# Last down projection of a decoder layer as seven block products, with the block sums of its weights added up in DRAM

## The chip, the core and the metric

The kernel runs on one core of a Trainium2 chip, as one program in float32 with split operands (below). The metric is the time of one execution on the device in microseconds.

## The reference, cut to what matters

The layer is SwiGLU feed-forward, mixers, SwiGLU feed-forward, each with RMS norms before and after and a residual. With 512 tokens, a width of 1024 and 2816 features, the last part is

```python
def swiglu(x, w_gate, w_up, w_down):
    return (jax.nn.silu(x @ w_gate) * (x @ w_up)) @ w_down

h = swiglu(rms_norm(x, ffn2_pre_norm[l]), ffn2_w_gate[l], ffn2_w_up[l], ffn2_w_down[l])
x = x + 0.5 * rms_norm(h, ffn2_post_norm[l])
```

The change concerns the product with `w_down` of this second feed-forward. Its left operand H is 512 x 2816, its right one 2816 x 1024.

## The kernel before, in words

Every float32 product is made of three TensorE matmuls: an operand x is split into `hi`, a copy cast to the format that TensorE reads, and `lo`, the rest x - hi; the product is hi.hi + lo.hi + hi.lo (`mm3`). ScalarE makes `hi` and VectorE makes `lo`, for weights in `wload` (L105 load by SP's queue, L106 cast, L109 rest) and for H in `split` (L122, L123).

The stages in order of time: the first feed-forward's gate and up products, its down projection, the mixers, the second feed-forward's gate and up products, its down projection, and the ending. In each gate-and-up stage most of the feature tiles run in `fast_phase` (16 of 22 tiles): for each tile gate and up are computed together as seven block products of 128x256 (`fast_prods`, matmuls on L437), on sums of weight blocks that VectorE makes in SBUF (`fast_load`, L403 to L417). The raw weights of a tile are four loads of 256 KB into one of two buffers `fq`; the split sums go into one of two sets (`fset`, and `fxth` with `fxtl`). The loads of tile f + 2 are issued as the buffer of tile f comes free.

The last down projection is plain: two parts of two token blocks (128 tokens each), each part with two column halves of 512, and each of these with 22 feature tiles (`down_half`). In the first column half of a part, H is split tile by tile as it is used. The weights are loaded again for each part, 4 x 22 loads of 256 KB. Six of them go through a small pool, the others through a ring of eight in the memory of two old tiles (`ringr`, `ringh`). The four sums of a part are in four PSUM banks. x, the residual, is loaded at the start of the stage by four DMAs of 512 KB, and the gain of the norm (`gb`) during the first part. `ending` takes the sums of one token block: two squares with row sums on ScalarE, two products with the gain and a chain of 128x1 instructions on VectorE, two updates of x (L171) and two stores (L172). In the second part, the second token block's last eight tiles come after the first block's last, so that the first block's ending runs beside them.

The order on each engine is that of the program, except that a scheduler moves instructions whose inputs are there earlier ahead of others by its own estimate. On the chip each engine then executes in that order, and an instruction that waits holds what is queued behind it. `order` adds to the scheduler's constraints that one instruction stands after another. A tile of a pool that reuses the memory of an older tile waits until every reader of the older one is done.

Of the kernel before, what the change touches and what calls it, by code (L numbers as in the profile page):

```python
# [10 lines left out]
F32 = mybir.dt.float32  # L11
# [6 lines left out]
P = 128  # L18
D = 1024
KT = 8  # L20
# [19 lines left out]
class Body:  # L40
# [74 lines left out]
    def mm3(self, out, lh, ll, rh, rl, first, last):  # L115
        t = self.nc.tensor
        t.matmul(out, lh, rh, start=first, stop=False)  # L117
        t.matmul(out, ll, rh, start=False, stop=False)  # L118
        t.matmul(out, lh, rl, start=False, stop=last)  # L119
# [299 lines left out]
    def fast_tile(self, f, S, T, banks, s7, H):  # L419
        g, up = self.fast_prods(S, T, banks, s7)  # L420
# [4 lines left out]
    def fast_prods(self, S, T, banks, s7, mid=()):  # L425
# [6 lines left out]
        def prod(out, w, t, start=False):  # L432
            th, tl = T[t]
            for k in range(4):
# [5 lines left out]
                m(wh, tl[:, k], start=False, stop=k == 3)  # L440
# [21 lines left out]
    def fast_phase(self, n, f0, xh, xl, RB, H, step):  # L462
# [12 lines left out]
        for f in range(f0 + 2, FT):  # L475
            i = f % 2
            self.fast_tile(f, self.sets[i], T, banks[i], s7[i], H)
# [37 lines left out]

    def load_x(self, src, x=None, after=None, tbs=range(TB), c=slice(0, D)):
# [9 lines left out]
    def order(self, later, earlier):  # L526
        d = mybir.DependencyInfo(mybir.DependencyClass.NoSync, mybir.DependencyReason.DATA)
# [645 lines left out]
    def run(self):  # L1173
# [3 lines left out]
        with tc.tile_pool(name="f1", bufs=1) as fp, contextlib.ExitStack() as x1:  # L1177
# [57 lines left out]
            with tc.tile_pool(name="st1", bufs=1) as st:  # L1235
# [4 lines left out]
                self.fast_phase(1, 4, xh, xl, RB, H, step)  # L1240
# [237 lines left out]
        with tc.tile_pool(name="f2", bufs=1) as fp, contextlib.ExitStack() as x1:  # L1478
# [26 lines left out]
            Hh, Hl, lor, gb = self.hidden_parts(x1, 2)  # L1505
            x = self.load_x(dx2)
            b4, c4 = self.bank8()
            self.ring = (self.cp.tile([P, KT, SEQ], F32, tag="xth", name="ringr"), self.cp.tile([P, KT, SEQ], F32R, tag="xtl", name="ringh"))
            self.ringi = -6
            parts = (((0, 1), [b4[:2], b4[2:]]), ((2, 3), [c4[:2], c4[2:]]))  # L1510
            lo4 = self.cp.tile([P, 4, 512], F32R, tag="mtl", name="lo4")
            lor += [lo4[:, i] for i in range(4)]
            for tbs, acc in parts:
                for h in range(2):
                    t0 = tbs[0] * P
                    step = (lambda k: self.hsplit(H, Hh, Hl, k, slice(t0, t0 + 256))) if h == 0 else None
                    self.down_half(Hh, Hl, "ffn2_d", FT, tbs, acc[h], h, lor if h and t0 else (), step, t0)
            self.post_gain("ffn2_post", 0.5 * self.RK, gb)
# [3 lines left out]
            for tbs, acc in parts:  # L1522
                for i, b in enumerate(tbs):
                    self.ending([acc[0][i], acc[1][i]], x, gb, b, self.out, tmp)
# [101 lines left out]
```

## Time and profile before

| | |
|---|---|
| median of 3 runs | 1325.09 us (1324.64 to 1326.45) |
| profiled execution, span from first to last instruction | 1326.1 us |
| TensorE busy | 1299.2 us, 98% |
| VectorE busy | 959.7 us, 72% |
| ScalarE busy | 738.6 us, 56% |
| GpSimd busy | 126.6 us, 10% |
| DMA | 178.35 MB, all but instruction loads from the queues of SP and ScalarE |

The profile gives no time of the profiled execution besides its span, which lies inside the range of the runs and 1.0 us above their median. Engine names in rows: PE is TensorE's matmuls, PEld its weight loads, DVE VectorE, ACT ScalarE, POOL GpSimd, SP SyncE, and a q behind a name is that engine's instruction queue or DMA issue. Lnnn is a line of the kernel.

### The profile page before, as it was taken

The page shows a single profiled execution, that of the slowest core. Times are in us where ns is not written, and L with a number is a line of the kernel's source. Part 1 is how long each engine was busy: PE and PEld are TensorE (multiplying, and loading weights), DVE is VectorE, ACT ScalarE, POOL GpSimd, SP SyncE. Part 2 cuts the span into 40 slices and gives each one's busy share as a digit, 9 for nine tenths or more (in the row PEclk, how much of TensorE's full clock was granted, in tenths as well). Part 3 has the DMA queues.
Part 4 walks back from the last instruction along what each step waited for, and adds up shares of the span by engine and source line. Part 5 has one row for each costly group of instructions (what it writes and reads, how often), then busy time and mean ns, then how long its engine had stood idle before and what let it go on. Part 6 is the DMA issues. An engine that isn't in the chain of part 4 may idle for free. (4 is left out here: it accounts for less than half of the span.)

```text
span 1326.1 us, 22368 instructions
## 1 busy us (share of the span) xinstructions
PE 1299.2 (98%) x8091; PEld 1129.2 (85%) x8091; DVE 959.7 (72%) x1860; ACT 738.6 (56%) x1591; POOL 126.6 (10%) x113
## 2 busy tenths in 40 slices
PE   8999999999999999999999999999999999999997
PEld 7889999888887778888777788888788999998886
DVE  6898786778567866755788766666687888756765
ACT  6566665767455644416565456444685566646642
POOL 0020000000001221102111121223100000000000
PEclk8999999999999999999999999999999999999999
DMA  7653331577664342234221242333744433318673
GB/s 241 194 162 113 111 112 49 167 258 246 200 181 125 97 114 72 80 107 120 64 56 57 64 135 65 96 96 112 277 148 155 141 107 114 111 33 277 195 226 104
DMA packets 106302, 178.35 MB, mean 134 GB/s; under 512 B 18780, under 2 KB 28368, under 8 KB 106192
## 3 DMA queue, kind: packets, MB, share of 16 engines
q1 hardware_dynamic: 105904, 176.67, 42.8%
q8 instruction: 63, 1.03, 0.3%
q10 hardware_dynamic: 288, 0.26, 0.1%
q14 instruction: 47, 0.39, 0.1%
HBM read 166.84 MB, written 10.01 MB: 133 GB/s over the span
## 5 line engine op out<-in xcount | busy, mean ns | idle before, releaser
L106 ACT CAST whi<-wraw 128x512 fp32r<-128x512 f32 (+1 forms) x286 | 173.6, 617 | 157.0 <-PE pfm L119 58.5
L109 DVE TENSOR_TENSOR wlo<-wraw,whi 128x512 fp32r<-128x512 f32 (+1 forms) x255 | 174.8, 694 | 70.3 <-ACT whi L106 65.7
L117 PE MATMUL pfm<-xth,whi 128*128 128x512 f32 x272 | 108.7, 405 | 0.9 <-DVE X L940 0.4
L118 PE MATMUL pfm<-xth,wlo 128*128 128x512 f32 x272 | 109.1, 406 | 0.0
L119 PE MATMUL pfm<-xtl,whi 128*128 128x512 f32 x272 | 108.3, 404 | 0.0
L106 ACT CAST ringh<-ringr 128x512 fp32r<-128x512 f32 x82 | 49.7, 621 | 42.9 <-DMA ringr<-in_ffn_d_dram 14.0
L437 PE MATMUL smm<-thi,fset 128*128 128x256 f32 x384 | 67.9, 276 | 0.0
L109 DVE TENSOR_TENSOR wlo<-ringr,ringh 128x512 fp32r<-128x512 f32 x75 | 51.3, 690 | 19.6 <-PE acc_e L119 8.0
L117 PEld LDWEIGHTS pfm<-xth,whi 128*128 128x128 f32 x272 | 51.3, 190 | 11.6 <-PE pfm L119 0.8
L109 POOL TENSOR_TENSOR wlo<-wraw,whi 128x512 fp32r<-128x512 f32 x28 | 38.1, 1360 | 229.2 <-ACT whi L106 165.1
L119 PEld LDWEIGHTS pfm<-xtl,whi 128*128 128x128 f32 x272 | 51.3, 190 | 9.8 <-issue 0.8
L118 PEld LDWEIGHTS pfm<-xth,wlo 128*128 128x128 f32 x272 | 51.3, 190 | 9.2 <-DVE wlo L109 0.4
L457 DVE TENSOR_TENSOR up<-s,smm 128x256 f32<-128x256 f32 x32 | 13.5, 422 | 61.8 <-ACT se L452 61.8
L437 PEld LDWEIGHTS smm<-thi,fset 128*128 128x128 f32 x384 | 57.9, 188 | 0.2
L437 PE MATMUL smm<-thi,fxtl 128*128 128x256 f32 x192 | 53.2, 277 | 0.6 <-DVE fxtl L412 0.6
L437 PE MATMUL smm<-thi,fxth 128*128 128x256 f32 x192 | 53.0, 276 | 0.0
L437 PE MATMUL se<-thi,fset 128*128 128x256 f32 x256 | 45.2, 276 | 0.0
L1058 ACT ACTIVATE Pm<-Pm,nm 128x384 f32<-128x384 f32 (+2 forms) x64 | 35.6, 558 | 14.5 <-DVE nm L1057 14.0
L123 DVE TENSOR_TENSOR Hl<-H,Hh 128x256 fp32r<-128x256 f32 x88 | 35.0, 421 | 8.6 <-ACT Hh L122 7.6
L403 DVE TENSOR_TENSOR fs<-fq 128x1024 f32<-128x1024 f32 x32 | 39.0, 1220 | 0.9 <-DMA fq<-in_ffn_u_dram 0.9
L437 PEld LDWEIGHTS se<-thi,fset 128*128 128x128 f32 x256 | 38.6, 188 | 0.0
L437 PEld LDWEIGHTS smm<-thi,fxtl 128*128 128x128 f32 x192 | 36.0, 188 | 1.0 <-DVE fxtl L412 1.0
(611 smaller groups left out, 4245.5 us busy)
## 6 DMA issues: line engine op xcount, KB each, us to landing
wraw<-in_ffn_d_dram SPq DMA_DIRECT2D x94, 256.0 KB, 2.8
ringr<-in_ffn_d_dram SPq DMA_DIRECT2D x82, 256.0 KB, 3.0
fq<-in_ffn_g_dram SPq DMA_DIRECT2D x64, 256.0 KB, 2.8
fq<-in_ffn_u_dram SPq DMA_DIRECT2D x64, 256.0 KB, 3.1
wraw<-in_ffn_g_dram SPq DMA_DIRECT2D x34, 256.0 KB, 3.2
wraw<-in_ffn_u_dram SPq DMA_DIRECT2D x34, 256.0 KB, 3.4
woraw<-in_w_out_dram SPq DMA_DIRECT2D x32, 256.0 KB, 4.4
mfq<-in_w_gate_dram SPq DMA_DIRECT2D x28, 256.0 KB, 3.0
```

What stands on the lines that cost most here:

```text
L106: nc.scalar.copy(hi, raw)
L109: eng.tensor_tensor(lo, raw, hi.bitcast(F32), op=OP.subtract)
L117: t.matmul(out, lh, rh, start=first, stop=False)
L118: t.matmul(out, ll, rh, start=False, stop=False)
L119: t.matmul(out, lh, rl, start=False, stop=last)
L123: return self.nc.vector.tensor_tensor(lo, src, hi.bitcast(F32), op=OP.subtract)
L403: add = lambda *x: v.tensor_tensor(*x, op=OP.add)
L437: m = lambda x, y, **kw: te.matmul(out, x, y, skip_group_check=True, **kw)
L457: v.tensor_tensor(up[:, 256:], s7, a, op=OP.subtract)
L1058: nc.scalar.activation(pm, pm, AF.Exp, bias=nm[:, qb : qb + 1], scale=-1.0, accum_out=sm[:, qb : qb + 1])
```

## The change

H and the weight W are cut into 2 x 2 blocks: token halves of 256, feature halves of 11 tiles, column halves of 512. Four sums T1 to T4 of weight blocks are made once, in DRAM, by DMAs issued from GpSimd: `weight_sums` lists eight steps, four plain copies and four that add into their destination, each cut into four pieces of 176 rows of 4 KB (704 KB). In the fast phase of the first feed-forward, a piece is handed out after the second and after the fifth product of each tile, with a wait for the last matmul of that product.

`down7` replaces the four `down_half` calls. It runs seven products of 256 tokens x 11 feature tiles x 512 columns. Three take a sum or difference of blocks of H as left operand: s3 into a buffer, s2 and s4 in place in H. Partial results move between PSUM banks by ScalarE copies, so that later products accumulate on them; two results are finished by VectorE additions into `c2` in SBUF. H is split in chunks of up to four tiles, the weights in pairs of tiles where they do not go through the small pool. The weights are now 7 x 11 tile loads, taken from W or from T1 to T4. x is loaded after the second product and the gain after the third, its second half with the sign turned. The endings of tokens 256 to 511 come after the sixth product, those of tokens 0 to 255 after the seventh.

```diff
@@ fast_prods
-                m(wh, tl[:, k], start=False, stop=k == 3)
+                self.mmark = m(wh, tl[:, k], start=False, stop=k == 3)
+            if side and w in (self.S_S3, self.S_S1):
+                side.pop(0)()
@@ fast_phase
-            self.fast_tile(f, self.sets[i], T, banks[i], s7[i], H)
+            self.fast_tile(f, self.sets[i], T, banks[i], s7[i], H, [side.pop(0) for _ in range(2) if side])
@@ new functions
+    def weight_sums(self, w, n):
+
+        g = self.nc.gpsimd
+        nh = self.a[w].shape[1] // 2
+        T = [self.dr.tile([nh, P, 512], F32, name=f"T{n}{i}") for i in range(4)]
+        v = lambda x: x.rearrange("k p n -> (k p n)").rearrange("(r c) -> r c", c=1024)
+        B = lambda i, j: v(self.a[w][j, nh * i : nh * i + nh])
+        t1, t2, t3, t4 = map(v, T)
+        todo = ((t1, B(0, 1), 0), (t3, B(1, 1), 0), (t1, B(0, 0), 1), (t3, B(0, 1), 1), (t2, t3, 0), (t2, B(0, 0), 1), (t4, t2, 0), (t4, B(1, 0), 1))
+
+        def piece(o, x, add, c):
+            i = g.dma_start(o[c], x[c], max_dma_last_dim=2048, **({"accum_op": OP.add} if add else {}))
+            self.order(i, self.mmark, mybir.DependencyClass.Sync)
+
+        r = nh * P // 8
+        return T, [lambda s=s, c=slice(r * j, r * j + r): piece(*s, c) for s in todo for j in range(4)]
+
+    def down7(self, H, w, T, x1, banks, done):
+
+        nc, v = self.nc, self.nc.vector
+        X, Y, Z, Q = banks
+        sh, sl = self.sring
+        sraw, q7, c2 = self.sraw, self.q7, self.c2
+        d = self.a[w]
+        nh = d.shape[1] // 2
+        h = lambda i, j, k, n: H[:, nh * j + k : nh * j + k + n, 256 * i : 256 * i + 256]
+        tt, st = v.tensor_tensor, v.scalar_tensor_tensor
+
+        def s3(k, n):
+            t = sraw[slot % 2][:, :n]
+            self.order(tt(t, h(0, 0, k, n), h(1, 0, k, n), op=OP.subtract), last)
+            return t
+
+        def s2(k, n):
+            a, q = h(0, 0, k, n), h(1, 0, k, n)
+            tt(q, h(1, 1, k, n), q, op=OP.subtract)
+            st(a, a, -1.0, q, op0=OP.mult, op1=OP.subtract)
+            return a
+
+        def s4(k, n):
+            a = h(0, 0, k, n)
+            st(a, a, -1.0, h(0, 1, k, n), op0=OP.mult, op1=OP.subtract)
+            return a
+
+        part = lambda i, j: lambda k, n: h(i, j, k, n)
+        seq = (
+            (X, d[0, :nh], part(0, 0), True),
+            (Q, T[2], s3, True),
+            (X, T[1], s2, False),
+            (Y, d[0, nh:], part(0, 1), False),
+            (Z, T[0], part(1, 0), False),
+            (X, T[3], part(1, 1), False),
+            (Z, d[1, nh:], s4, False),
+        )
+        slot = wslot = 0
+        last = None
+        wr, wh_, wl_ = self.wring
+
+        def weights(m, src, k):
+            nonlocal wslot
+            if m == 0 and k < 6:
+                return {k: self.wload(src[k])}
+            n = 2 if (nh - k) % 2 == 0 else 1
+            raw, hi, lo = wr[wslot % len(wr)][:, :n], wh_[wslot % len(wh_)][:, :n], wl_[wslot % len(wl_)][:, :n]
+            wslot += 1
+            nc.sync.dma_start(raw, src[k : k + n].rearrange("k p n -> p k n"))
+            nc.scalar.copy(hi, raw)
+            tt(lo, raw, hi.bitcast(F32), op=OP.subtract)
+            return {k + i: (hi[:, i], lo[:, i]) for i in range(n)}
+
+        for m, (acc, src, make, start) in enumerate(seq):
+            ops, ws = {}, {}
+            cuts = (0, 1, 4, 8, nh) if m == 0 else (0, 4, 8, nh)
+            lag = 8 if m == 6 else 0
+
+            def mm(i, k):
+                t = slice(i * P, i * P + P)
+                hi, lo = (o[:, t] for o in ops[k])
+                wh, wl = ws[k]
+                e = lambda a, b, s, f: nc.tensor.matmul(acc[i], a, b, start=s, stop=f, skip_group_check=True)
+                e(hi, wh, start and k == 0, False)
+                e(lo, wh, False, False)
+                self.mmark = e(hi, wl, False, k == nh - 1)
+
+            for k in range(nh):
+                if k in cuts:
+                    n = cuts[cuts.index(k) + 1] - k
+                    hi, lo = sh[slot % 4][:, :n], sl[slot % 4][:, :n]
+                    slot += 1
+                    f = make(k, n)
+                    nc.scalar.copy(hi, f)
+                    last = tt(lo, f, hi.bitcast(F32), op=OP.subtract)
+                    ops.update({k + i: (hi[:, i], lo[:, i]) for i in range(n)})
+                if k not in ws:
+                    ws.update(weights(m, src, k))
+                for i in range(1 if k >= nh - lag else 2):
+                    mm(i, k)
+            if lag:
+                for k in range(nh - lag, nh):
+                    mm(1, k)
+            for i in range(2):
+                if m == 0:
+                    nc.scalar.copy(Y[i], X[i])
+                elif m == 1:
+                    nc.scalar.copy(q7[:, i], Q[i])
+                elif m == 2:
+                    nc.scalar.copy(Z[i], X[i])
+                elif m == 4:
+                    tt(c2[:, 1, i], Z[i], q7[:, i], op=OP.add)
+                elif m == 5:
+                    tt(c2[:, 0, i], X[i], q7[:, i], op=OP.add)
+            done(m)
+
@@ first feed-forward
-                self.fast_phase(1, 4, xh, xl, RB, H, step)
+                self.T2, side = self.weight_sums("ffn2_d", 2)
+                self.fast_phase(1, 4, xh, xl, RB, H, step, side)
@@ last down projection
-            Hh, Hl, lor, gb = self.hidden_parts(x1, 2)
-            x = self.load_x(dx2)
+            dw = x1.enter_context(self.tc.tile_pool(name="dw2", bufs=1))
+            gb = dw.tile([P, 2, 512], F32, name="gb")
+            self.sraw = [dw.tile([P, 4, 256], F32, name=f"sraw{i}") for i in range(2)]
+            self.q7 = dw.tile([P, 2, 512], F32, name="q7")
+            self.c2 = dw.tile([P, 2, 2, 512], F32, name="c2")
+            lor = [dw.tile([P, 2, 512], F32R, name=f"lor{i}") for i in range(4)]
+            self.wx = None
+            dv = x1.enter_context(self.tc.tile_pool(name="dv2", bufs=1))
+            ch = lambda nm: dv.tile([P, 4, 256], F32R, name=nm)
+            sh2 = ch("sh2")
+            dv.tile([P, 64], F32, name="gap")
+            sh3, sl2, sl3 = ch("sh3"), ch("sl2"), ch("sl3")
+            dv.tile([P, 64], F32, name="gap2")
+            dv = x1.enter_context(self.tc.tile_pool(name="dz2", bufs=1))
+            sl0, sl1, sh0, sh1 = ch("sl0"), ch("sl1"), ch("sh0"), ch("sh1")
+            self.sring = [sh0, sh1, sh2, sh3], [sl0, sl1, sl2, sl3]
+            x = []
             b4, c4 = self.bank8()
-            self.ring = (self.cp.tile([P, KT, SEQ], F32, tag="xth", name="ringr"), self.cp.tile([P, KT, SEQ], F32R, tag="xtl", name="ringh"))
-            self.ringi = -6
-            parts = (((0, 1), [b4[:2], b4[2:]]), ((2, 3), [c4[:2], c4[2:]]))
+            banks = b4[:2], c4[:2], c4[2:], b4[2:]
+            rings = [self.cp.tile([P, KT, SEQ], t, tag=g, name=n) for t, g, n in ((F32, "xth", "ringr"), (F32R, "xtl", "ringh"))]
             lo4 = self.cp.tile([P, 4, 512], F32R, tag="mtl", name="lo4")
-            lor += [lo4[:, i] for i in range(4)]
-            for tbs, acc in parts:
-                for h in range(2):
-                    t0 = tbs[0] * P
-                    step = (lambda k: self.hsplit(H, Hh, Hl, k, slice(t0, t0 + 256))) if h == 0 else None
-                    self.down_half(Hh, Hl, "ffn2_d", FT, tbs, acc[h], h, lor if h and t0 else (), step, t0)
-            self.post_gain("ffn2_post", 0.5 * self.RK, gb)
+            two = lambda x: [x[:, i : i + 2] for i in range(0, x.shape[1], 2)]
+            self.wring = two(rings[0]), two(rings[1]), lor + two(lo4)
             pre = self.cp.tile([P, 4, 512], F32, tag="mth", name="pre")
             pre = iter([pre[:, i % 4] for i in range(8)])
             tmp = lambda: next(pre)
-            for tbs, acc in parts:
-                for i, b in enumerate(tbs):
-                    self.ending([acc[0][i], acc[1][i]], x, gb, b, self.out, tmp)
+
+            def done(m):
+                if m == 1:
+                    x.extend(self.load_x(dx2, after=self.mmark))
+                if m == 2:
+                    i = self.nc.sync.dma_start(gb.rearrange("p h d -> p (h d)"), self.a["ffn2_post"].partition_broadcast(P))
+                    self.order(i, self.mmark)
+                    for h in range(2):
+                        nc.vector.tensor_scalar(gb[:, h], gb[:, h], 0.5 * self.RK * (1, -1)[h], None, op0=OP.mult)
+                if m == 5:
+                    for i in range(2):
+                        self.ending([self.c2[:, 0, i], self.c2[:, 1, i]], x, gb, 2 + i, self.out, tmp)
+                if m == 6:
+                    for i in range(2):
+                        self.ending([banks[1][i], banks[2][i]], x, gb, i, self.out, tmp)
+
+            self.down7(H, "ffn2_d", self.T2, x1, banks, done)
 
 
 def host_layout(i):
```

In a piece, `self.order(i, self.mmark, Sync)` is a wait on the chip, where the other uses of `order` only fix the scheduler's order.

## Rows read from the trace of the kernel before

**Rows 1.** The page's first part: busy us, share of the span and instructions of an engine.

```profile
PE 1299.2 (98%) x8091; PEld 1129.2 (85%) x8091; DVE 959.7 (72%) x1860; ACT 738.6 (56%) x1591; POOL 126.6 (10%) x113
```

**Rows 2.** The stages one by one: length, busy us and instructions of each engine, granted clock, share of the DMA engines, GB/s. In order: gate and up of the first feed-forward, its down projection with what follows, gate and up of the second, its down projection, the tail.

```profile
85.50:242.00 156.50, 155.76 (x1353) 155.01 (x1351) 118.36 (x141) 91.29 (x188) 2.55 (x1) 1.00 0.31 97
242.00:371.00 129.00, 127.87 (x587) 105.08 (x588) 93.71 (x202) 85.60 (x181) 2.08 (x4) 1.00 0.74 230
1048.00:1198.00 150.00, 149.58 (x1312) 149.38 (x1310) 112.89 (x136) 86.62 (x178) 0.00 (x0) 1.00 0.31 99
1198.00:1318.40 120.40, 120.30 (x528) 98.88 (x528) 85.11 (x169) 67.89 (x143) 0.00 (x0) 1.00 0.68 205
1318.40:1326.10 7.70, 0.00 (x0) 0.00 (x0) 3.30 (x10) 0.69 (x2) 0.00 (x0) 0.74 0.29 110
```

**Rows 3.** The timeline of TensorE's matmuls at the start and the end of the last down projection: start, us, engine, line, operation, count, and in brackets the idle time before and what ended it.

```profile
1197.30 0.28 PE L437 MATMUL se<-txb,fxth 128*128 128x256 f32 x1
1198.00 0.73 PE L117 MATMUL acc_mm<-whi,Hh 128*128 128x512 f32 x2 [0.42 <-ACT Hh L122]
...
1317.75 0.39 PE L118 MATMUL acc_s<-ringh,Hl 128*128 128x512 f32 x1
1317.98 0.39 PE L119 MATMUL acc_s<-lo,Hh 128*128 128x512 f32 x1
```

**Rows 4.** DMA traffic from 100 to 209 us, inside the first fast gate-and-up stage: all packets, the queue of SP, and one of its two groups of loads with KB each and median us to landing.

```profile
DMA packets 6636, 12.23 MB, mean 112 GB/s; under 512 B 736, under 2 KB 736, under 8 KB 6624
q1 hardware_dynamic: 6624, 12.06, 34.8%
fq<-in_ffn_u_dram SPq DMA_DIRECT2D x24, 256.0 KB, 2.8
```

**Rows 5.** The timeline of VectorE and ScalarE around the start of the last down projection; a row with x2 or more is a run of instructions back to back.

```profile
1171.37 1.22 DVE L403 TENSOR_TENSOR fs<-fq 128x1024 f32<-128x1024 f32 x1
1172.50 1.22 DVE L417 TENSOR_TENSOR fset<-fq,fset 128x1024 fp32r<-128x1024 f32 x1
...
1181.72 1.23 DVE L417 TENSOR_TENSOR fxtl<-fq,fxth 128x1024 fp32r<-128x1024 f32 x1 [0.69 <-ACT fxth L416]
...
1202.26 3.11 DVE L123 TENSOR_TENSOR Hl<-H,Hh 128x256 fp32r<-128x256 f32 x9
...
1207.81 1.29 DVE L109 TENSOR_TENSOR wlo<-ringr,ringh 128x512 fp32r<-128x512 f32 x2
...
1201.37 3.17 ACT L122 CAST Hh<-H 128x256 fp32r<-128x256 f32 x10
...
1206.93 1.14 ACT L106 CAST ringh<-ringr 128x512 fp32r<-128x512 f32 x2
```

**Rows 6.** Waits between 1196 and 1326 us: engine and line that waited, for whom, us in total, times, the longest. The first row is all that TensorE waited.

```profile
PE acc_mm L117 <- ACT Hh L122: 0.4, 1, 0.4
...
DVE gb L254 <- DMA gb<-in_ffn_post_dram: 2.5, 1, 2.5
```

**Rows 7.** DMA traffic from 1190 to 1326.1 us: GB/s in 40 slices, and two groups of loads.

```profile
GB/s 0 199 247 379 402 319 233 229 306 159 274 191 222 179 117 243 196 214 211 183 163 236 230 302 339 187 202 194 217 172 195 194 210 164 0 0 2 154 0 154
...
ringr<-in_ffn_d_dram SPq DMA_DIRECT2D x82, 256.0 KB, 3.0
xa<-dx SPq DMA_DIRECT2D x2, 512.0 KB, 4.2
```

**Rows 8.** The timeline of GpSimd from 60 to 371 us: its last instruction in the first gate-and-up stage and the next one after it.

```profile
83.96 4.08 POOL L308 TENSOR_TENSOR sg<-sg,RB 128x256 f32<-128x256 f32 x1 [8.42 <-ACT sg L304]
307.70 1.84 POOL L933 MEMSET X<- 128x1024 f32 x2 [219.66 <-DVE Hl L123]
```

**Rows 9.** The timeline of SP, ScalarE and VectorE in the first fast stage: the ends of two tiles (L422), the last of the four loads of a tile (L406), the first use of that tile's weights (L409), the end of their conversion (L412), and the last load of the stage.

```profile
189.52 0.35 SPq L406 DMA_DIRECT2D fq<-in_ffn_u_dram  x1
...
208.65 0.39 SPq L406 DMA_DIRECT2D fq<-in_ffn_u_dram  x1
...
193.77 0.60 ACT L422 ACTIVATE sg<-se 128x512 f32<-128x512 f32 x1 [0.75 <-PE se L437]
...
195.45 0.63 ACT L409 CAST fxth<-fq 128x512 fp32r<-128x512 f32 x1
...
203.35 0.60 ACT L422 ACTIVATE sg<-se 128x512 f32<-128x512 f32 x1 [0.75 <-PE se L437]
...
202.97 1.75 DVE L412 TENSOR_TENSOR fxtl<-fq,fxth 128x1536 fp32r<-128x1536 f32 x1
```

**Rows 10.** The timeline of the ending of the last token block.

```profile
1318.46 0.60 ACT L164 ACTIVATE junk<-acc_s 128x512 bf16<-128x512 f32 x1 [4.23 <-PE acc_s L119]
...
1319.18 0.69 DVE L165 TENSOR_TENSOR pre<-acc_s,gb 128x512 f32<-128x512 f32 x1 [1.49 <-ACT junk L164]
...
1321.31 1.41 DVE L171 SCALAR_TENSOR_TENSOR xb<-pre,r1y,xb 128x512 f32<-128x512 f32 x2
```

More of the change, by code (lines that the diff above doesn't have):

```diff
@@ L118, in mm3 @@
         t.matmul(out, ll, rh, start=False, stop=False)
-        t.matmul(out, lh, rl, start=False, stop=last)
+        self.mmark = t.matmul(out, lh, rl, start=False, stop=last)
     def split(self, hi, lo, src):
@@ L417, in fast_load, with fast_tile @@
             v.tensor_tensor(lo[:, c], x, hi[:, c].bitcast(F32), op=OP.subtract)
-    def fast_tile(self, f, S, T, banks, s7, H):
-        g, up = self.fast_prods(S, T, banks, s7)
+    def fast_tile(self, f, S, T, banks, s7, H, side=()):
+        g, up = self.fast_prods(S, T, banks, s7, side=side)
         sg = self.tp.tile([P, SEQ], F32, tag="tmpa", bufs=2, name="sg")
@@ L423, in fast_tile, with fast_prods @@
         self.nc.vector.tensor_tensor(H[:, f], sg, up, op=OP.mult)
-    def fast_prods(self, S, T, banks, s7, mid=()):
+    def fast_prods(self, S, T, banks, s7, mid=(), side=()):
         nc, v, te = self.nc, self.nc.vector, self.nc.tensor
@@ L460, in fast_prods, with fast_phase @@
         return g, up
-    def fast_phase(self, n, f0, xh, xl, RB, H, step):
+    def fast_phase(self, n, f0, xh, xl, RB, H, step, side=()):
         quads, sums, s7 = self.fr
@@ L524, in load_x, with order @@
         return x
-    def order(self, later, earlier):
-        d = mybir.DependencyInfo(mybir.DependencyClass.NoSync, mybir.DependencyReason.DATA)
+    def order(self, later, earlier, how=mybir.DependencyClass.NoSync):
+        d = mybir.DependencyInfo(how, mybir.DependencyReason.DATA)
         self.tc.add_manual_dep(getattr(later, "ins", later), getattr(earlier, "ins", earlier).name, d, reason="order")
```

## The prediction

> **What bounds the kernel now.** I read the page's busy times first. TensorE is busy for nearly the whole span and GpSimd for a tenth of it [rows 1]. A busy TensorE proves little by itself, so the stages come next [rows 2]: in both fast gate-and-up stages and in the last down projection the TensorE column is within 1 us of the length of the stage, at the full granted clock (1.00, the 2.4 GHz level), while VectorE is busy 71 to 76% and ScalarE 56 to 58%. The timeline of TensorE at both ends of the down projection shows it without holes [rows 3]: a gap of 0.42 us before its first matmul, then one matmul on the next until 1318.37. So this stage is bound by the number of its matmuls: 120.30 us for 528, or 0.2278 us each, and what feeds them has room. Behind it lies a tail of 7.7 us with no matmul, the ending of the last token block [rows 10].
>
> **Fewer matmuls.** Before, there are 22 feature tiles x 4 token blocks x 2 column halves x 3 = 528 matmuls of 512 columns. After, 7 products x 11 tiles x 2 token blocks x 3 = 462 of the same shape. 66 x 0.2278 = 15.0 us less, all of it on the path that sets the end, as long as the operands come in time. The bounds of this term are narrow, since shape and clock do not change.
>
> **The start of the stage.** The 0.42 us before the first matmul is a wait for the cast of H [rows 3, 6], which stood behind other work. Now the first chunk of H has split buffers in the space of the raw weights, free once the weights of the last tile have been converted at 1182.95, some 14 us earlier [rows 5]. I take 0.4 us as gained; the bounds are 0 and 0.6.
>
> **VectorE in the down projection.** Back to back, instructions start closer than their duration: one of 256 elements each 0.34 us ((3.11 - 0.42)/8), of 512 each 0.60 (1.29 - 0.69), of 1024 each 1.13 (1172.50 - 1171.37) [rows 5]; scalar_tensor_tensor of 512 each 0.66 [rows 10], so 1.24 for 1024 by the same ratio. Products 2 to 7 each split weights in five pairs and a single, 5 x 1.13 + 0.60 = 6.25, and H in chunks of 4, 4 and 3 tiles, 1.13 + 1.13 + 0.87 = 3.13: 9.4 us. The first product takes 9.7 (7 x 0.60 + 2 x 1.13 for weights, 3.2 for four chunks). The formed operands add 3.1 us (product 2), 3.1 + 3.4 (product 3, two instructions per chunk) and 3.4 (product 7). Four sums into c2 cost 2.4, and two endings (tokens 256 to 511) now fall inside product 7: 0.6 + 3.5 us each by the last ending [rows 10], 8.2 in all. Together 9.7 + 56.4 + 13.0 + 2.4 + 8.2 = 89.7 us of 105.2, 85%, where before it was 71%. On totals VectorE does not become the bound.
>
> The tight place is product 3. By its last chunk VectorE must have done 9.7 + 12.5 + 15.9 = 38.1 us, and TensorE asks for that chunk at 2 x 15.0 + 8 x 6 x 0.2278 = 41.0 us after the start. That leaves 2.9 us, plus about 3.0 done ahead (chunks of one and three tiles, three weights). An operand goes VectorE, ScalarE, VectorE, so some of it goes in hand-overs. ScalarE needs 7.8 us per product (1024 elements at 0.94, from 0.31 for 256 and 0.52 for 512 [rows 5]) and two PSUM copies of 0.6 [rows 9]: no bound in 15.
>
> **Moved DMAs.** Weights stay at 77 x 256 KB = 20.2 MB in 105 us, 192 GB/s against the 205 of the stage now [rows 2]. Moved into it are the four loads of x (2.1 MB, issued before the weights until now), put on SP's queue after product 2, and the gain, after product 3. What stands behind them on SP are the weight loads. At the best rate in a slice, 402 GB/s, x takes 5.2 us [rows 7]; the weight rings hold four pairs, eight tiles, 8 x 1.37 = 10.9 us of matmuls. So it is hidden, and costs up to 5 us without that cover. The gain's scaling on VectorE waited 2.5 us for its DMA before [rows 6], with splits queued behind it; this can recur, after product 3, where VectorE has 5 us per product to spare. For all supply together the bounds are 0 and 9 us; I take 1.0, nearer to zero because the sums leave 5.9 us at the tightest place.
>
> **The weight sums in the first stage.** 32 pieces of 704 KB, two in each of 16 tiles of 9.58 us (193.77 to 203.35) [rows 9]; 16 are copies, 16 add into DRAM. They add no work to TensorE, VectorE or ScalarE. Each waits on GpSimd for a matmul, and nothing else is queued there before 307.7 us, 66 us after the stage [rows 8]. They share the DMA engines with the weight loads. The trace has no transfer from DRAM to DRAM and none that adds, so I bound them by the loads. Loads average 112 GB/s here [rows 4] and reach 402 [rows 7], so they need 28% or 2.7 us of a tile and leave 6.9. A tile's two pieces are 1.44 MB, 3.6 us at that rate. From below a copy costs one such load and an add two; from above (read and write one after the other) a copy costs two and an add three. Over 16 tiles that is 8 x 3.6 + 8 x 7.2 = 86 us or 8 x 7.2 + 8 x 10.8 = 144; the room is 16 x 6.9 + 8 = 118 (no loads in the last three tiles, the last being issued at 208.65 [rows 9]). The middle, 1.5 and 2.5, makes 115: it just fits.
>
> A load that comes late is covered twice. The last of a tile's four, issued at 189.52, lands 2.8 us later at 192.3 and is first used at 195.45, 3.1 us on; the conversion ends at 204.72, while the set is wanted at about 212.9, one tile after 203.35 [rows 4, 9]: 8.2 us of cover on TensorE. In tiles that add, the middle is 2.7 + 9.0 - 9.6 = 2.1 us over, 17 over eight tiles if no copying tile between gave anything back. I take 1.5 us of loss, bounds 0 and 25.
>
> The Trainium skill (Collectives: The Full Stack, "The bandwidth ceiling: the fold count and why AG ≠ RS ≠ AR") says that an add in the DMA engine needs two source reads on one ring and runs at half the rate of a copy. No row here shows an adding transfer; by that page and a copy at 1.5 loads, an add would cost 3, the sum would be 130 us of an estimated room of 118, and the rule speaks for the second and third rivals below.
>
> **The tail.** Two endings of four leave the last stretch or stay covered as before; the last block's chain after the last matmul is the same, 7.7 us: nothing.
>
> **Sum.** 1326.1 - 15.0 - 0.4 + 1.0 + 1.5 = 1313.2 us of span. The profiled span is 1.0 above the median of the runs, 1325.09, so I forecast 1312.2.
>
> **Rivals.** First, the down projection is fed late: hand-overs idle VectorE by another tenth (38.1 becomes 41.9, past 41.0), x and the gain fall into the same products, and 6 us of stalls appear about product 3. For it speaks 85% of busy time, against it that no wait of TensorE but one of 0.4 us shows today [rows 6]. 1312.2 - 1.0 + 6 = 1317. Chance 15%.
>
> Second, the pieces run over. At three loads for an add and 1.5 for a copy, 12 us of transfers are left at the end of the gate-and-up stage, and the first down projection uses 74% of the engines already [rows 2]; 12/0.26 is 46 us of sharing, of which I price about 6 us as stalls: 1317 to 1318. Chance 12%.
>
> Third, on the other side: the adding pieces hold the engines and the loads are served behind them. A tile that adds then lasts 2.7 + 3.6p, p being the price of an add in loads, and eight of them lose 8 x (3.6p - 6.9) - 8.2. At p = 3 that is 23 us, and the copies at two loads 2 more: 1312.2 - 1.5 + 25 = 1336, slower. It decides from a loss of 15 us, p = 2.7. Against it: four loads need only 2.7 of 9.58 us, so half of the engines' time would do. Chance 10%. The Trainium skill (DMA: Bandwidth & Descriptors, "Queues, rings and completion order") says that each engine takes packets in turn from the queues that have work; this would keep the loads going and turn the third rival into the second, and no run here shows two busy queues.
>
> **How the numbers follow.** Forecast 60%, its own range 1309 to 1315.5 (supply and contention between 0 and 6 together); rivals 15, 12 and 10%; 3% for anything else. The range of 8 in 10 is 1309 to 1323: below, every stall is zero, the start gains all and half a microsecond is left for the spread of the runs; above, it takes in both milder rivals and leaves the third out. A change of under 0.2% (2.6 us) cannot be told from none. Faster by more: 60 + 14 + 9 = 83%; within: 5% (the upper parts of the first two rivals); slower: 10 + 2 = 12%.
>
> **What would show it.** Right: 462 matmuls from the start of the last down projection, 0.228 us apart, some 106 us long; VectorE at about 85% there; no wait of TensorE above 1 us about product 3; both sides of the first gate-and-up stage where they were, 85.5 and 242 us, with a DMA share near 1 in it and the added queue idle by about 250 us. Wrong: TensorE waiting there for converted weights, a first down projection longer than its 129 us with loads landing much later than 3 us, or holes between the seven products. The prediction is most exposed to the price of an adding transfer, which no row gives.

## The result

The changed kernel takes 1323.38 us (20 runs, 1318.57 to 1330.39), where the kernel before, run beside it, took 1330.12 (20 runs, 1324.52 to 1336.94). The ratio is 0.9949 [0.9931, 0.9968], or 6.8 us [4.2, 9.1] less of the 1325.09 shown above. The forecast was 1312.2, or 12.9 less, with a range of 1309 to 1323: the result lies 0.4 us above its top. Of the 11.2 us between forecast and result, 5.0 lie in the kernel before, which read higher in this comparison, and 6.1 in what the change saved.

The page of the changed kernel, busy us, the new queue, and the pieces issued from GpSimd (count, KB, median us to landing; the row has the 24 that read W, and the other eight read a sum):

```profile
span 1320.0 us, 21997 instructions
PE 1286.8 (97%) x8025; PEld 1118.4 (85%) x8025; DVE 968.8 (73%) x1812; ACT 735.7 (56%) x1532; POOL 151.7 (11%) x145
q0 software_dynamic: 8960, 23.07, 7.8%
T<-in_ffn_d_dram POOLq DMA_DIRECT2D x24, 704.0 KB, 8.3
```

Its stages by the columns of [rows 2] (us, busy PE, PEld, DVE, ACT, POOL, granted clock, DMA share, GB/s), in the same order:

```profile
85.50:248.90 163.40, 158.22 (x1347) 157.11 (x1345) 117.46 (x138) 90.78 (x187) 25.98 (x33) 1.00 0.88 227
249.03:381.30 132.27, 128.35 (x584) 104.36 (x585) 93.84 (x202) 85.10 (x180) 2.08 (x4) 1.00 0.74 228
1064.10:1207.20 143.10, 143.10 (x1257) 143.10 (x1256) 106.75 (x127) 82.46 (x169) 0.00 (x0) 1.00 0.28 89
1207.25:1312.40 105.15, 105.14 (x464) 86.45 (x462) 93.21 (x121) 64.57 (x84) 0.00 (x0) 1.00 0.64 214
1312.40:1320.00 7.60, 0.00 (x0) 0.00 (x0) 3.30 (x10) 0.69 (x2) 0.00 (x0) 0.83 0.30 116
```

The last down projection is 105.15 us with TensorE busy throughout: 15.2 less than its 120.37 before [rows 2, 3], as forecast (of the 464 matmuls in its row, two began before the window). The loss is at the other end of the kernel. The two fast phases by their tiles' ends (ScalarE, count, ns, first and last start in us), first in the kernel before, then in the changed one:

```profile
L422 ACT ACTIVATE sg<-se x16: 592/600/600, 98.4 to 241.9; 128x512 f32<-128x512 f32 x16
L422 ACT ACTIVATE sg<-se x16: 592/600/600, 1054.3 to 1197.9; 128x512 f32<-128x512 f32 x16
```

```profile
L422 ACT ACTIVATE sg<-se x16: 593/599/602, 97.2 to 248.9; 128x512 f32<-128x512 f32 x16
L422 ACT ACTIVATE sg<-se x16: 588/600/600, 1064.1 to 1207.6; 128x512 f32<-128x512 f32 x16
```

The first phase, in which the pieces run, grew from 143.5 to 151.7 us; the second, without pieces, kept its 143.6. The first down projection after it grew from 128.4 to 132.3. The books of the two spans: -1.2 ahead of the first phase, +8.2 in it, +3.8 in the first down projection, -1.0 in the mixers, -0.5 at the start of the last down projection (its wait of 0.42 us [rows 3] is gone), -15.2 in it, -0.1 in the tail: -6.1 but for rounding, which is 1326.1 to 1320.0.

What TensorE waited for in the changed kernel, the three longest rows (us in total, times, longest):

```profile
PE smm L437 <- ACT ss L450: 4.5, 3, 2.4
PE acc_mm L117 <- ACT whi L106: 2.0, 1, 2.0
PE pu L117 <- ACT whi L106: 2.0, 1, 2.0
```

The first row is new and stands in the first phase; the second is also new and stands 8 us into the first down projection; the third lies before both and is no news (3.0 us in the kernel before). One of the three waits of the first row, in the timeline of SP, GpSimd, VectorE, ScalarE and TensorE (start, us, engine, line, operation; in brackets the idle time before and what ended it):

```profile
142.26 0.54 SPq L406 DMA_DIRECT2D fq<-in_ffn_u_dram  x1
...
143.73 0.93 POOL L529 DMA_DIRECT2D T<-in_ffn_d_dram  x1 [3.26 <-PE smm L437]
...
151.23 1.23 DVE L403 TENSOR_TENSOR fs<-fq 128x1024 f32<-128x1024 f32 x1 [2.36 <-issue]
...
152.49 0.62 ACT L416 CAST fset<-fs 128x512 fp32r<-128x512 f32 x1 [2.69 <-DVE fs L403]
153.02 0.37 ACT L450 ACTIVATE ss<-smm 128x256 f32<-128x256 f32 x1
...
153.44 0.50 PE L437 MATMUL smm<-thi,fset 128*128 128x256 f32 x2 [1.89 <-ACT ss L450]
```

And the same place in the kernel before, where the copy was on line 448:

```profile
141.59 0.39 SPq L406 DMA_DIRECT2D fq<-in_ffn_u_dram  x1
...
148.36 1.22 DVE L403 TENSOR_TENSOR fs<-fq 128x1024 f32<-128x1024 f32 x1
...
149.61 0.62 ACT L416 CAST fset<-fs 128x512 fp32r<-128x512 f32 x1 [0.24 <-DVE fs L403]
150.14 0.37 ACT L448 ACTIVATE ss<-smm 128x256 f32<-128x256 f32 x1
```

Read it from below. TensorE waits for the copy that turns the sign of a PSUM sum (`u <- -a`). The copy needs nothing that is late; it stands in ScalarE's queue behind the cast of `fs`, weights that TensorE wants only a tile later. The cast waits for VectorE's addition, and that waits for a load which was issued 9.0 us earlier (142.26 to 151.23). The row of the addition names no releaser (`issue`); that it is the load is read from the load's semaphore, whose last update the trace has at 151.15, 8.9 us after the issue. Before, the load had landed after 3.1 us, and the addition came 6.8 us after the issue, when VectorE got round to it. So the load had 6.8 us of cover, and behind that next to nothing: in the three tiles that wait, loads of 8.9, 9.6 and 7.6 us came out as waits of TensorE of 1.9, 2.4 and 0.3 us, through an in-order queue.

The wait in the first down projection is also one for a late load, here of weights that TensorE wants next. ScalarE's cast waits 4.2 us for them, while the last add, issued at 246.19, is still on its way (it lands after 9.1 us):

```profile
255.62 1.14 ACT L106 CAST whi<-wraw 128x512 fp32r<-128x512 f32 x2 [4.20 <-DMA wraw<-in_ffn_d_dram]
...
256.81 0.50 PE L117 MATMUL acc_mm<-whi,Hh 128*128 128x512 f32 x1 [2.02 <-ACT whi L106]
```

What a piece costs, in two stretches of the changed kernel: copies from 89 to 129 us, adds from 129 to 170 (queue: packets, MB, share of 16 engines; then us to landing):

```profile
q0 software_dynamic: 1536, 5.77, 42.1%
q1 hardware_dynamic: 2458, 4.48, 35.7%
T<-in_ffn_d_dram POOLq DMA_DIRECT2D x8, 704.0 KB, 5.5
fq<-in_ffn_u_dram SPq DMA_DIRECT2D x8, 256.0 KB, 4.5
```

```profile
q0 software_dynamic: 2634, 5.17, 74.2%
q1 hardware_dynamic: 2258, 4.12, 28.7%
T<-in_ffn_d_dram POOLq DMA_DIRECT2D x8, 704.0 KB, 9.6
fq<-in_ffn_u_dram SPq DMA_DIRECT2D x8, 256.0 KB, 7.1
```

The packets of a MB of copies take the 16 engines 0.421 x 40 / 5.77 = 2.9 us, of adds 0.742 x 41 / 5.17 = 5.9, of loads 3.2 and 2.9 here and 0.348 x 109 / 12.06 = 3.1 in the kernel before [rows 4]. So a copy costs 0.9 of the load before and an add 1.9, where I took 1.5 and 2.5. But I had counted the load at the best rate of a slice, 402 GB/s or 2.5 us per MB, which made 3.7 us of a copy and 6.2 of an add: the copy was too dear, the load too cheap, and the add nearly right. The Trainium skill (Collectives: The Full Stack, "The bandwidth ceiling: the fold count and why AG ≠ RS ≠ AR") has the add, there the reducing step of a ring of cores, at half the rate of a copy: the trace agrees, 5.9 to 2.9. A tile of adds holds 1.44 MB x 5.9 + 1.05 MB x 2.9 = 11.5 us of packets and lasts 9.6, so it runs over by some 2 us, as the prediction had it (2.1); the shares of the two queues add up to 103%. The copies that follow land after 7.5, 6.4, 6.2 and 5.8 us: there it is worked off. Meanwhile the loads beside adds land after 7.1 us in the median, the latest after 9.6, and the cover is 6.8.

### The profile page after: what moved, and what is told of

Read it like the earlier page. It is cut to its first block, busy times and chain, and to the rows that moved or that the text cites. A ratio compares the mean times of both kernels' runs of the same rounds, so it can differ in the third digit from the quotient of the medians.

```text
span 1320.0 us, 21997 instructions
## 1 busy us (share of the span) xinstructions
PE 1286.8 (97%) x8025; PEld 1118.4 (85%) x8025; DVE 968.8 (73%) x1812; ACT 735.7 (56%) x1532; POOL 151.7 (11%) x145
## 3 DMA queue, kind: packets, MB, share of 16 engines
q0 software_dynamic: 8960, 23.07, 7.8%
## 5 line engine op out<-in xcount | busy, mean ns | idle before, releaser
L584 ACT CAST ringh<-ringr 128x1024 fp32r<-128x1024 f32 (+1 forms) x39 | 37.8, 975 | 27.3 <-PE acc_s L597 6.5
L1173 ACT ACTIVATE Pm<-Pm,nm 128x384 f32<-128x384 f32 (+2 forms) x64 | 35.6, 558 | 14.5 <-DVE nm L1172 13.9
L409 ACT CAST fset<-fq 128x512 fp32r<-128x512 f32 x48 | 29.6, 620 | 12.5 <-PE ss L437 5.9
L437 PEld LDWEIGHTS smm<-thi,fxth 128*128 128x128 f32 x192 | 36.0, 188 | 0.4 <-ACT ss L450 0.4
```

Of the source, the lines that this page charges most:

```text
L409: nc.scalar.copy(hi[:, i], q[:, i])
L437: m = lambda x, y, **kw: te.matmul(out, x, y, skip_group_check=True, **kw)
L584: nc.scalar.copy(hi, raw)
L1173: nc.scalar.activation(pm, pm, AF.Exp, bias=nm[:, qb : qb + 1], scale=-1.0, accum_out=sm[:, qb : qb + 1])
```

## The experiments

**One part alone.** My theory (A): the seven products give their 15 us, and the pieces cost some 12, through late loads that reach TensorE by ScalarE's queue. The rival (B): the products also fall short, or the pieces cost by something else. First the pieces in the kernel before, with the sums not read by anything:

```diff
  (kernel before, with weight_sums, mmark and side as in the change)
-                self.fast_phase(1, 4, xh, xl, RB, H, step)
+                self.T2, side = self.weight_sums("ffn2_d", 2)
+                self.fast_phase(1, 4, xh, xl, RB, H, step, side)
```

> The kernel before, with the 32 pieces issued in the first gate-and-up stage as in the change and their sums never read; the last down projection stays plain. Theory A (the pieces delay the weight loads, and ScalarE's queue then holds a PSUM copy that TensorE needs): the stage grows from 143.5 us between the first and last tile to about 152, the first down projection by 3 to 4 us, and the kernel is 10 to 13 us slower than before. Rival B (the missing microseconds are not the pieces' doing, but the clock, the matmul pitch or the spread of executions): within 2 us of before.

1338.33 us, ratio 1.0083 [1.0054, 1.0112]: 11 us [7, 15] slower. TensorE's waits in its first phase and down projection:

```profile
PE smm L437 <- ACT ss L450: 5.6, 3, 2.7
PE acc_mm L117 <- ACT whi L106: 1.8, 1, 1.8
```

The same two waits, without the seven products; the first phase is 152.5 us. Then the products without the pieces:

```diff
-                self.T2, side = self.weight_sums("ffn2_d", 2)
-                self.fast_phase(1, 4, xh, xl, RB, H, step, side)
+                d2 = self.a["ffn2_d"]
+                self.T2 = [d2[0, :11], d2[0, 11:], d2[1, :11], d2[1, 11:]]
+                self.fast_phase(1, 4, xh, xl, RB, H, step)
```

> The changed kernel without the pieces: the seven products read blocks of the weights as they are where they would read T1 to T4, so the weight sums are left out of the computation. Theory A: the first gate-and-up stage is as before (143.5 us), the last down projection lasts 105 us, and the kernel is 15 to 16.5 us faster than before. Rival B: about 7 us faster, as the changed kernel, since the down projection or the clock takes the rest.

1311.31 us, ratio 0.9885 [0.9861, 0.9909]: 15.2 us less. The two parts add up to -4.2, and the change measured -6.8, the same within the intervals.

**Copies or adds.** The kernel before with the same 32 pieces, each of them a plain copy:

```diff
-            i = g.dma_start(o[c], x[c], max_dma_last_dim=2048, **({"accum_op": OP.add} if add else {}))
+            i = g.dma_start(o[c], x[c], max_dma_last_dim=2048, **{})
```

> As the pieces alone on the kernel before, with every adding piece made a plain copy of the same bytes; nothing reads the results. Theory A with the price in the adds (in the changed kernel a copying piece landed after about 5.5 us and an adding one after 9): the loads land after about 4 us, TensorE does not wait in the tiles, and the kernel is 0 to 4 us slower than before. Rival C (the mere presence of a second busy queue costs, whatever it does): 8 us or more slower, like the pieces with adds.

1328.94 us, ratio 1.0018 [0.9997, 1.004]: 0 to 5 us, for the same 23.07 MB. Its queue, and the landing of the pieces and of loads:

```profile
q0 software_dynamic: 6144, 23.07, 5.1%
T<-in_ffn_d_dram POOLq DMA_DIRECT2D x24, 704.0 KB, 5.8
fq<-in_ffn_u_dram SPq DMA_DIRECT2D x64, 256.0 KB, 3.8
```

Its first phase is 143.6 us and no wait for the copy stands in it. So it is the adds that cost, and not the bytes on the queue. The last load of a tile lands 3.3 to 6.0 us after its issue in that phase, within the cover. That it is the lateness of loads, and not something else in an add, is the question of the next run.

**The order on ScalarE.** The changed kernel with the second half of a tile's conversion, VectorE's additions and ScalarE's casts of the sums, put behind the copy of the running tile (ScalarE's lines 450 and 416 above are then 464 and 428, VectorE's 403 is 421):

```diff
+    def fast_rest(self, S, X, after=None):   # second half of fast_load, from the adds on
 ...
+                i1 = nc.scalar.copy(hi[:, c.start + j], x[:, j])
+                if after is not None:
+                    self.order(i1, after)
@@ fast_prods
-        nc.scalar.activation(u, a, AF.Copy, scale=-1.0)
+        neg = nc.scalar.activation(u, a, AF.Copy, scale=-1.0)
+        if self.rest:
+            self.rest(neg)
+            self.rest = None
```

> The changed kernel, with the casts of the summed weights of a tile put behind the negating PSUM copy (L450) of the tile that then runs, on ScalarE, in both fast stages. Theory A: a late load no longer holds that copy, the waits of TensorE for it (4.5 us) go, the stage is 3.5 to 5 us shorter than in the changed kernel, and the kernel is 10 to 12 us faster than before; the loads land as late as in the changed kernel. Rival D (the loads are late for the conversion itself, whatever stands in the queue): the wait moves to the weights of the next tile and the time is that of the changed kernel, some 7 us below before.

1317.07 us, ratio 0.992 [0.9898, 0.9942]: 10.6 us less than before. Its first phase as one window, its pieces and loads from 129 to 170 us, and what TensorE still waits for behind it:

```profile
97.90:241.50 143.60, 143.29 (x1257) 143.10 (x1255) 106.29 (x127) 81.09 (x172) 23.47 (x30) 1.00 0.93 241
```

```profile
T<-in_ffn_d_dram POOLq DMA_DIRECT2D x8, 704.0 KB, 10.2
fq<-in_ffn_u_dram SPq DMA_DIRECT2D x8, 256.0 KB, 7.2
```

```profile
PE acc_mm L118 <- ACT whi L107: 2.9, 1, 2.9
```

This run decides between order and bandwidth. The adds and the loads are as late as in the changed kernel, the DMA engines are busier (0.93), and the phase is 143.6 us, as if there were no pieces. So the waits came from the order on the engines, not from the bandwidth, and rival D is out. But the edit did two things, as one load and the addition that uses it show:

```profile
153.76 0.38 SPq L407 DMA_DIRECT2D fq<-in_ffn_u_dram  x1
```

```profile
163.14 1.22 DVE L421 TENSOR_TENSOR fs<-fq 128x1024 f32<-128x1024 f32 x1
```

The addition now comes 9.4 us after its load is issued, where it came 6.8 before, so the cover is longer too. Two loads of the phase landed later than that, after 9.7 and 10.0 us, and cost TensorE nothing; most landed within it. How much is due to the freed queue and how much to the longer cover is not separated. In time the run is 3.8 us more saved than by the changed kernel, which is the size of the waits (4.5), but the two intervals overlap. The first down projection keeps its loss (133.7 us): there the last adds stand beside the first weights. Over all thirteen profiles of this document, that projection is 131.7 to 133.7 us in the four in which the last add lands 6 to 8 us behind the phase, each with a wait of 1.8 to 2.9 us for a weight cast, and 128.0 to 130.4 in the nine others, without that wait.

**One piece per tile.** The changed kernel with 16 pieces in each of the two fast phases:

```diff
-            if side and w in (self.S_S3, self.S_S1):
+            if side and w == self.S_S3:
@@ fast_phase
-... [side.pop(0) for _ in range(2) if side])
+... [side.pop(0) for _ in range(1) if side])
@@ run
-                self.fast_phase(2, 4, xh, xl, None, H, step)
+                self.fast_phase(2, 4, xh, xl, None, H, step, self.side)
```

> One piece per tile, after the second product, in the 16 tiles of the first fast phase and the 16 of the second; all else as in the changed kernel. Theory A (a load beside adding transfers lands late, and the ScalarE copy that TensorE needs is queued behind the cast that waits for it; and adds that end after the stage slow the weights of the first down projection): a tile then holds one add of some 8 us and no second one behind it, loads land in 4 to 5.5 us, and the waits of TensorE for that copy shrink from 10 us to under 2; the first down projection keeps at most two adding pieces. Some 1314 us where the kernel before takes 1327, 12 to 14 less. Theory B (an adding transfer costs a fixed amount wherever it runs beside compute): 16 adds cost the same 11 to 12 us, only split over two stages, and the kernel takes some 1320, 7 less than before.

1314.69 us where before took 1335.68 beside it, ratio 0.9873 [0.984, 0.9907]: 16.8 us [12, 21] less, as much as the products give alone. Its first phase is 143.9 us, its first down projection 128.0. (The changed kernel's waits for the copy are 4.5 us, not the 10 that this expectation and a later one name.) Late and spread together:

> One piece per tile over both fast phases, and the casts that wait for the loads ordered behind the copy that TensorE needs. Theory A: nothing is left of the contention in the fast phases (tiles 9.58 us, no wait for that copy), and at most 1 us in the first down projection: 1311 to 1313 where before takes 1327, as much as the seven products give alone (15.2 less). Theory B (fixed cost of each add): as with late casts alone, some 1317, 10 less. If it is no better than the spread alone, the order of the casts no longer matters once loads are no later than 5 us.

1318.43 us, ratio 0.9886 [0.9854, 0.9918], no different from the spread alone within these intervals. In the profile of the spread kernel the last load of a tile lands at most 7.6 us after its issue, 0.8 past the cover, and TensorE has no wait for the copy left that the order could remove. Theory B, a fixed cost of each add, is out by both.

**In the mixers.** All pieces between the tasks of the two mixers:

```diff
+            if every and n % every == every - 1 and self.side:   # in tasks(), every=4
+                self.side.pop(0)()
```

> All 32 pieces are issued between the tasks of the two mixers, one in four tasks, each behind the last matmul before it; the first fast phase has none, and its tiles must be 9.58 us again and the first down projection as short as before (128 us). The unknown is the mixers: GpSimd has its own work there and a piece takes 0.6 to 0.95 us of its issue, so up to 26 us of GpSimd spread over 680 us, and a queue in which work stands behind the pieces' waits. Theory A (only where a load's lateness reaches an in-order engine within a tile does an add cost anything): the mixers lose 0 to 4 us, 1312 to 1316 where before takes 1327. Theory B (fixed cost of each add): some 1320. A third way: the mixers' chains of small dependent steps have less cover than the fast phase, and they lose over 8 us: 1320 or more, with waits of TensorE for GpSimd's results or for late loads in the mixers.

1341.57 us, ratio 1.0049 [1.0021, 1.0078]: the third way, worse than either kernel, where theory A had 0 to 4 us of loss. The first phase is 143.6 us, but the stretch from the first down projection's end to the second phase's first tile end went from 683.8 to 709.9. TensorE's longest waits there, and three windows of the mixers:

```profile
PE ptk L804 <- DVE Bi L870: 6.2, 1, 6.2
PE pfm L118 <- POOL wlo L109: 4.3, 1, 4.3
```

```profile
455.00:540.00 85.00, 77.08 (x437) 65.07 (x436) 54.49 (x137) 33.01 (x76) 22.92 (x26) 0.96 0.48 128
540.00:625.00 85.00, 79.03 (x493) 63.80 (x492) 47.15 (x138) 21.92 (x68) 11.14 (x13) 0.94 0.57 131
625.00:710.00 85.00, 79.68 (x424) 61.43 (x423) 59.95 (x184) 47.91 (x123) 27.37 (x27) 0.98 0.64 177
```

The DMA engines have room here, and it does not help: TensorE is idle for 19 of these 255 us, and its mean granted clock is below 1.00. In the kernel before it was idle for 4.5 of the same 255 us, at 1.00. Two things changed at once, GpSimd's queue, in which pieces that wait for a matmul (twelve such waits make 76.6 us, the longest 28.3) stand ahead of its weight splits, and the loads; no run separates them.

**Profiled again.** In the changed kernel the waits for the copy, 4.5 us, make the tiles that hold them 5.1 us longer. Another 3.0 of the phase's 8.2 us are ten tiles (97.16 to 146.14 us and 198.87 to 248.88) whose matmuls last 281 ns instead of 276 and start 0.118 us apart instead of 0.114, with a granted clock of 1.00 and, but for 0.5 us, nothing to wait for. Four kernels were profiled once more for that.

> The kernel before, profiled a second time. Within the fast phases a 128x256 matmul lasts 276 ns in most profiles and 281 ns in some stretches of 20 to 140 us (in the changed kernel, with pieces only, and in the second phase of both spread kernels), with the granted clock read as 1.00 in both cases; a tile is then 9.90 us and not 9.58. Theory C (the stretches belong to phases in which pieces add into DRAM): none here. Theory D (they come and go with the execution, whatever the kernel): they may stand anywhere, here too.

> The changed kernel, profiled a second time. The waits of TensorE for the ScalarE copy behind the late cast come again, some 10 us in the first fast phase, as they belong to the order of the program; the first down projection is 131 to 133 us. Theory C: stretches of 281 ns in the first fast phase, none in the second. Theory D: anywhere or nowhere.

> One piece per tile in both fast phases, profiled a second time. No wait of TensorE above 0.6 us in the phases again. Theory C: stretches of 281 ns in the second phase again (and none in the mixers or in the last down projection). Theory D: elsewhere or none.

> One piece per tile and casts ordered behind the copy, profiled a second time. Its second phase stood at 281 ns throughout, 148.2 us for 143.6. Theory C: again. Theory D: 276 ns there, 143.6 us, and a span of some 1308.5.

One run of each: 1326.55, 1324.48, 1314.94 and 1310.85 us, the kernel before beside them 1331.11. The kernel before: 276 ns, but for the first 3 us of each phase (below). The changed kernel: the wait for the copy again (4.5 us, in two waits), the first phase 151.7 us, the first down projection 132.9, and 281 ns from 180 to 217 us, where the first profile had it from 86 to 142 and from 205 on. The spread kernel: one stretch of 10 us in its first phase, which had none before, and none in its second, which had 75 us of them. The late and spread one: none, where its second phase had been at 281 throughout, as here in that first profile (count, ns, first and last start):

```profile
L451 PE MATMUL smm<-thi,fset x160: 281/281/281, 1064.8 to 1187.5; 128*128 128x256 f32 x160
```

Stretches of some 10 us and more at 281 ns stand in 6 of the 12 phases that hold adds and in none of the 14 that hold none. But every fast phase, of every kernel, is at 281 ns for its first 3 us, as in the kernel before:

```profile
L437 PE MATMUL smm<-thi,fset x7: 281/281/281, 87.5 to 88.6; 128*128 128x256 f32 x7
```

In three of the six phases that pace was only not left: in the changed kernel it stands from 86 us on, while its first piece is issued at 89.34 and its first add at 129.66. So neither theory as put. The stretches come and go with the execution, in phases that hold adds and not only beside the adds; the one phase with copies alone has none. What makes them is open.

The second profile of the changed kernel shows one thing more. Behind its longer wait, 2.8 us, the granted clock fell to 0.50, the level of 1.2 GHz:

```profile
176.04 0.80 PE L437 MATMUL smm<-thi,fset 128*128 128x256 f32 x2 [2.76 <-ACT ss L450]
```

```profile
175.50:178.90 3.40, 2.85 (x13) 2.86 (x14) 1.31 (x2) 1.63 (x4) 0.00 (x0) 0.50 0.83 289
```

Matmuls then start 0.21 us apart, and the tile takes 14.0 us instead of 9.6: the wait of 2.8 us cost 4.4. The pieces alone show the same behind a wait of 2.4 us (a tile of 13.9), but not behind one of 2.7, and in the first profile of the changed kernel the clock stayed at 1.00 behind waits of 1.9 and 2.4. So such a wait costs its own length, and in two of these five cases 1.6 and 1.8 times it.

## Why the prediction was wrong, and where it was right

- **Fewer matmuls, -15.0:** right. -15.2 in the spans, -15.2 in the products alone.
- **Start of the stage, -0.4:** -0.5. **Tail, 0:** -0.1.
- **Supply of the last down projection, +1.0 (0 to 9):** 0, as TensorE waited for nothing there; the first rival is out. VectorE is at 93.2 of 105.15 us, 89% where the sum had 85.
- **The price of a transfer:** the copy too dear and the load too cheap, as shown above; the add was nearly right, and so was the 2.1 us by which a tile of adds runs over. The second rival's three loads for an add did not hold, but its end came in part: the last add landed 6.4 us behind the phase, beside the first down projection's weights, and that stage lost 3.8 us where the rival had priced 6.
- **The third rival:** its side did not come true. Loads beside adds land after 7 us, not behind them. The Trainium skill (DMA: Bandwidth & Descriptors, "Queues, rings and completion order") has engines take packets in turn from the queues with work, and the landing times are in line with it: 256 KB loads of 7.1 us beside adds of 9.6.
- **Contention, +1.5 (0 to 25):** this is the step that failed. It measured 8.2 in the phase and 3.8 behind it, 12.0 in all, within its bounds but eight times the value taken. The value rested on "a load that comes late is covered twice". The first cover, until VectorE uses the load, was real, and 6.8 us after the issue in the row above. The second, 8.2 us until TensorE wants the converted set, was not: it is the cover of the set, not of what stands behind its cast in ScalarE's queue. The rows that I read [rows 9] show the loads and the conversions of a tile and leave out the PSUM copies between them; two lines of ScalarE's timeline in the kernel before (149.61 and 150.14 above) would have shown cast and copy back to back. I had asked what is queued behind a late instruction for GpSimd and SP, and not for ScalarE. This accounts for the 5.1 us of the tiles that wait. The 3.8 us are the second rival's effect, to which the value gave nothing; the 3.0 us of the second pace nothing in the prediction stood for, and their cause is open.

The 10.5 us that this term was short, less the supply not needed (1.0), 0.4 at the last down projection's start, length and tail, and 2.2 by which the spans differ ahead of the first phase and in the mixers, make the span's excess of 6.8 (1320.0 against 1313.2) but for rounding.

## What to carry to other kernels

A transfer added to a stage whose DMA engines have room was priced here by how late it made the loads, not by its bytes: compare a load's time from issue to first use with its landing time beside the new traffic. Cover ends at the first in-order engine that waits: list what stands behind the waiting instruction on its queue, and if something there is wanted sooner than the late data, order it ahead. Thinning out the transfers (one add per tile instead of two) saved 16.8 us [12, 21], mending the order 10.6 [8, 14]: the intervals overlap, but only the first also relieved the stage behind.

## What the runs showed of the hardware

- An add from DRAM into DRAM (704 KB) took 9.6 us to land beside loads, a copy of the same size 5.5; per MB the adds kept the engines busy for 5.9 us, the copies 2.9, loads from DRAM to SBUF 2.9 to 3.2.
- The share of the DMA engines was 0.93 over 143.6 us with TensorE idle for 0.3 of them (late casts); a share near 1 was no sign of loss by itself.
- The granted clock fell to 0.50 behind a wait of TensorE of 2.8 us, and the tile lost 4.4 us (changed kernel, second profile).
- Matmuls of 128x256 have a second pace, 281 ns for 276, at a granted clock of 1.00: for the first 3 us of every fast phase, and for some 10 us and more only in phases with adds. I had no expectation of it, and its cause is not known.
